# Strassen's seven products in the first feed-forward matrix of a diffusion backbone step

## The chip, the cores and the metric

One core of a Trainium2 chip. TensorE multiplies (weights are loaded into it, the tokens stream past and the sums land in PSUM), VectorE and ScalarE do the elementwise work and alone of the two sides read PSUM, gpsimd (POOL in the profile) does elementwise work in SBUF and issues some DMAs, and SyncE (SP) issues the others. The metric is the time of one execution on the device in microseconds; lower is better.

## The reference, cut to what matters

Two trunk layers over 640 tokens (512 of a latent grid and 128 of context), 1024 features. A layer is a feed-forward half-step, a token-mixing step (state-space scan, attention, gated MLP) and a second feed-forward half-step; each is preceded by a norm with modulation vectors worked out from a condition.

```python
D_MODEL, SEQ, DEC_SEQ, DEPTH, D_FF = 1024, 128, 512, 2, 2816
def swiglu_ffn(h, w_in, w_out):
    gate, up = jnp.split(h @ w_in, 2, axis=-1)      # w_in: 1024 x 5632, "the first matrix"
    return (jax.nn.silu(gate) * up) @ w_out
def adaln(cond, w_ada, b_ada):
    mod = jax.nn.silu(cond) @ w_ada + b_ada
    return mod.reshape(cond.shape[0], N_MOD, D_MODEL)
def trunk_layer(x, mod, lp, ctx_kv, ssm_init):
    h = modulate(rmsnorm(x, lp['norm_ffn1']), sh1, sc1)
    x = x + 0.5 * g1 * swiglu_ffn(h, lp['ffn1_w_in'], lp['ffn1_w_out'])
    h = modulate(rmsnorm(x, lp['norm_mix']), sh2, sc2)
    mix, ctx_state = token_mixing(h, lp, ctx_kv, ssm_init)
    x = x + g2 * mix
    h = modulate(rmsnorm(x, lp['norm_ffn2']), sh3, sc3)
    x = x + 0.5 * g3 * swiglu_ffn(h, lp['ffn2_w_in'], lp['ffn2_w_out'])
    return x, ctx_state
```

So there are four feed-forward stages: layer 0 first and second, layer 1 first and second. They are called the first to the fourth (or last) stage here.

## The kernel before, in words

Features lie on the 128 partitions, tokens along the columns. The 640 tokens are two halves, `HALF` (line 27): A has 384, B has 256. Float32 accuracy comes from three passes: every operand is kept as a high part in the matmul's format and a low part (the remainder), and `mm3` (line 361) issues high by high, high by low and low by high, at lines 365 to 367. The splitting is `split_h` (line 188): ScalarE writes the high part (line 191), VectorE subtracts it from the source (line 192). Normed tokens are in `H`, high and low.

A feed-forward stage (`ffn_items`, line 566) goes by 22 units of 128 hidden features. For a unit and a half, `in_task` (line 598) runs eight tiles of 128 features for the gate, ScalarE takes its SiLU out of PSUM (line 610), eight tiles for the up part follow, VectorE multiplies (line 619) and the result is split into `hid`. Units come in four blocks, `BLOCKS` (line 30), of 5, 5, 6 and 6. After a block's units (its *in-phase*) come its `out_task`s (line 681; the *out-phase*): for each of eight output tiles and each half, the block's units are multiplied by the second matrix and `accumulate` (line 389) adds the result, times its gate vector, to the residual `x` on VectorE (line 395; A is one range of columns, B two).

The order of all engines' instructions is laid down at build time. `run` (line 92) walks a list of tasks; `clock` (line 80) advances a clock `T` of the matrix work by a set length for each `mm3` (`MM3`, line 44) and lets background generators go on when their time on that clock has come. Weights come in chunks of 1024 columns (512 KB): `dma` (line 110) loads them on SP's queue into two raw buffers, `split` (line 125) splits them into one of seven buffers, at most 24 units of `T` ahead of use (`LEAD`), 4.5 while a norm is under way (`LEAD_HOT`).

In the background of the first three stages run: `ada` (line 237), which works out modulation vectors with two VectorE instructions of 1024 columns a step (line 260), at a pace in `T` given in `build` (4.5 then 7.0 in the first stage, 48 steps; 4.5 then 6.5 in the second, 56 steps; 10.0 in the third, 24 steps; none in the fourth); and in the first and third `ssm_build` (line 774), which works out tables of the state-space part on VectorE and gpsimd and sends them to memory with gpsimd's DMAs. `norm` (line 297) runs, tile by tile, when a half's residual is done: VectorE and gpsimd scale, ScalarE shifts and rounds, VectorE takes the remainder. `square` (line 284) sums squares on ScalarE and gpsimd. At the very start, `opening` (line 405) loads the tokens and works out the first norm, with modulation on VectorE (line 449) and gpsimd (line 469) side by side, while `lead_task` (line 638) runs the first two units feature tile by feature tile. PSUM has four banks for products (tag `mm`) and two each of two small tags.

## Time and profile before

| | us |
|---|---|
| median of 3 runs | 2525.57 (2521.89 to 2526.12) |
| the profiled execution, span | 2522.3 |
| first stage, 85 to 534.5 | 449.5 |
| second stage, 824 to 1290 | 466 |
| third stage, 1290 to 1768 | 478 |
| fourth stage, 2054 to 2522 | 468 |
| mixing steps | 289.5 and 286 |

The profile is of one execution. Times count from its first instruction. A *window* gives each engine's busy time in a stretch, with the granted clock of TensorE (1.00 is full speed). A line of the list of instruction groups gives line, engine, operation, output and inputs by the program's names, shape, count, busy time with the mean of one in ns, and the idle time ahead of it with what ended it. A line of the timeline gives start and duration of instructions in order of time. A busy span on VectorE counts a wait of an instruction that has been started; a matmul's span includes its way through the array, so that successive ones overlap.

### The profile page before, as it was taken

To read this page: it belongs to the slowest core of one execution; us is meant where nothing else is said; L and a number is where in the kernel's file an instruction comes from. 1 tells how busy PE (TensorE), PEld (TensorE's weight loads), DVE (VectorE), ACT (ScalarE), POOL (GpSimd) and SP (SyncE) were. 2 spreads that over 40 slices of the span, in tenths; PEclk is the share of its full clock that TensorE was granted. 3 is DMA by queue.
4 is the path that set the end of the run, shared out by engine and by line. 5 is a ranking of instruction groups with operands and counts; after the bars stand their busy time and mean duration, and the time that the engine had idled before them with its cause. 6 is when DMAs were issued, how large, how long until landed. Compare 5 with 4: busy or idle time off the path is not lost.

```text
span 2522.3 us, 44229 instructions
## 1 busy us (share of the span) xinstructions
PE 2466.4 (98%) x17428; PEld 2408.2 (95%) x17428; DVE 1555.2 (62%) x3293; ACT 812.4 (32%) x1689; POOL 680.9 (27%) x1520
## 2 busy tenths in 40 slices
PE   6999999999999999999999999999999999999999
PEld 5999999998988999999999999999998889999999
DVE  7798777557566776666568675534685764343332
ACT  5322222254444422222242222223545452222121
POOL 5105765623342000000020566551253320000000
PEclk8999999999999999999999999999999999999999
DMA  6445454325341344443324344332444212222222
GB/s 229 144 147 170 159 168 164 109 110 148 121 129 46 127 172 142 151 148 144 117 86 144 134 150 151 105 98 74 143 149 122 82 54 91 74 85 67 83 68 67
DMA packets 102115, 307.29 MB, mean 122 GB/s; under 512 B 21666, under 2 KB 24834, under 8 KB 101524
## 3 DMA queue, kind: packets, MB, share of 16 engines
q1 hardware_dynamic: 86548, 254.92, 29.8%
q0 software_dynamic: 15360, 49.56, 6.2%
q8 instruction: 137, 2.24, 0.4%
q14 instruction: 70, 0.57, 0.1%
HBM read 281.78 MB, written 23.17 MB: 121 GB/s over the span
## 4 chain that ended last, share of the span: by engine, by line
PE 87%; DVE 5%; issue 3%; ACT 2%; POOL 1%; DMA 1%; SPq 0%; DVEq 0%; POOLq 0%; ACTq 0%
PE mm L365 26%; PE mm L367 26%; PE mm L366 26%; PE mm L1389 1%; PE mm L1390 1%; PE mm L1391 1%; DVE aj L449 1%; DVE w L192 1%; PE sA L1258 1%; PE sB L1280 1%; PE mm L1227 1%; DMA T<-dT 0%; DVE H L541 0%; PE sB L1093 0%; PE sA L909 0%
## 5 line engine op out<-in xcount | busy, mean ns | idle before, releaser
L365 PE MATMUL mm<-H,w 128*128 128x384 f32 (+1 forms) x3248 | 1021.3, 314 | 9.5 <-ACT H L536 5.6
L366 PE MATMUL mm<-H,w 128*128 128x384 f32 (+1 forms) x3248 | 1011.9, 312 | 12.3 <-DVE H L541 9.3
L367 PE MATMUL mm<-H,w 128*128 128x384 f32 (+1 forms) x3248 | 1011.3, 311 | 0.0
L365 PEld LDWEIGHTS mm<-H,w 128*128 128x128 f32 x3248 | 615.0, 189 | 21.9 <-issue 13.8
L366 PEld LDWEIGHTS mm<-H,w 128*128 128x128 f32 x3248 | 615.1, 189 | 15.5 <-DVE H L541 11.1
L367 PEld LDWEIGHTS mm<-H,w 128*128 128x128 f32 x3248 | 614.7, 189 | 1.1 <-DVE w L192 1.1
L192 DVE TENSOR_TENSOR w<-r,w 128x1024 fp32r<-128x1024 f32 (+2 forms) x354 | 395.5, 1119 | 243.7 <-ACT w L191 242.3
L365 PE MATMUL mm<-hid,w 128*128 128x384 f32 (+1 forms) x1408 | 434.4, 309 | 0.0
L367 PE MATMUL mm<-hid,w 128*128 128x384 f32 (+1 forms) x1408 | 433.5, 308 | 0.0
L366 PE MATMUL mm<-hid,w 128*128 128x384 f32 (+1 forms) x1408 | 432.9, 307 | 0.0
L191 ACT ACTIVATE w<-r 128x1024 fp32r<-128x1024 f32 (+2 forms) x354 | 337.8, 956 | 289.8 <-PE mm L367 232.5
L260 DVE SCALAR_TENSOR_TENSOR aj<-ar,sbc 128x1024 bf16<-128x1024 f32 x256 | 317.4, 1240 | 36.4 <-DMA ar<-w_ada 32.4
L395 DVE SCALAR_TENSOR_TENSOR x<-mm,mod,x 128x128 f32<-128x128 f32 (+1 forms) x480 | 194.0, 434 | 183.7 <-PE mm L367 183.0
L365 PEld LDWEIGHTS mm<-hid,w 128*128 128x128 f32 x1408 | 264.1, 188 | 1.0 <-issue 1.0
L366 PEld LDWEIGHTS mm<-hid,w 128*128 128x128 f32 x1408 | 264.7, 188 | 0.0
L367 PEld LDWEIGHTS mm<-hid,w 128*128 128x128 f32 x1408 | 264.5, 188 | 0.0
L191 ACT ACTIVATE hid<-sg 128x384 fp32r<-128x384 f32 (+1 forms) x176 | 82.9, 471 | 550.4 <-DVE sg L619 534.5
L295 POOL TENSOR_TENSOR acc<-acc,sq 128x384 f32<-128x384 f32 (+1 forms) x60 | 53.7, 895 | 604.8 <-ACT sq L293 604.1
L619 DVE TENSOR_TENSOR sg<-sg,mm 128x256 f32<-128x256 f32 (+1 forms) x161 | 78.1, 485 | 212.0 <-PE mm L367 211.9
L610 ACT ACTIVATE sg<-mm 128x256 f32<-128x256 f32 (+1 forms) x161 | 70.0, 435 | 329.7 <-PE mm L367 329.7
L192 DVE TENSOR_TENSOR hid<-sg,hid 128x384 fp32r<-128x384 f32 (+1 forms) x176 | 89.2, 507 | 94.6 <-ACT hid L191 94.6
L1389 PE MATMUL mm<-w,H 128*128 128x256 f32 x480 | 143.1, 298 | 0.0
(329 smaller groups left out, 2642.2 us busy)
## 6 DMA issues: line engine op xcount, KB each, us to landing
ar<-w_ada SPq DMA_DIRECT2D x128, 512.0 KB, 4.5
r<-f1i SPq DMA_DIRECT2D x88, 512.0 KB, 3.4
r<-f0i SPq DMA_DIRECT2D x86, 512.0 KB, 3.5
r<-f0o SPq DMA_DIRECT2D x32, 384.0 KB, 3.1
r<-wqkv SPq DMA_DIRECT2D x24, 512.0 KB, 3.5
r<-f1o SPq DMA_DIRECT2D x32, 384.0 KB, 3.0
r<-f0o SPq DMA_DIRECT2D x32, 320.0 KB, 2.9
r<-f1o SPq DMA_DIRECT2D x32, 320.0 KB, 2.9
```

The source lines that it names most:

```text
L191: self.nc.scalar.activation(hi, src, AF.Copy)
L192: self.nc.vector.tensor_tensor(lo, src, hi.bitcast(F32), op=ALU.subtract)
L260: nc.vector.scalar_tensor_tensor(jk, r, 1.0, self.sbc[:, c, :], op0=ALU.mult, op1=ALU.mult, accum_out=m[:, c, j * KD + k:j * KD + k + 1])
L295: eng.tensor_tensor(self.acc[X], self.acc[X], q, op=ALU.add)
L365: nc.tensor.matmul(out, hi, rhs_hi, start=start, stop=False)
L366: nc.tensor.matmul(out, hi, rhs_lo, start=False, stop=False)
L367: nc.tensor.matmul(out, lo, rhs_hi, start=False, stop=stop)
L395: nc.vector.scalar_tensor_tensor(self.x[:, m, r0:r1], p[:, r0 - s:r1 - s], self.mod[l][:, c, g * KD + m:g * KD + m + 1], self.x[:, m, r0:r ...
L449: v.scalar_tensor_tensor(jk, r, 1.0, self.sbc[:, c, :], op0=ALU.mult, op1=ALU.mult, accum_out=m[:, c, j:j + 1])
L610: nc.scalar.activation(sg[:, :e - s], p[:, :e - s], AF.Silu)
L619: nc.vector.tensor_tensor(sg[:, :e - s], sg[:, :e - s], p[:, :e - s], op=ALU.mult)
L1389: nc.tensor.matmul(p[:, :256], H[:, 0, k, ts], wh, start=k == 0, stop=False)
```

## The change

The first matrix of a feed-forward stage is multiplied by Strassen's scheme (in Winograd's form): the two halves of the 1024 features, the two halves of the tokens and the pair of gate and up are the two-by-two blocks. In place of eight block products for a unit (gate and up, two feature halves, two token halves) there are seven, each of four feature tiles of 128 by 320 token columns.

- Halves are both 320 tokens (`HT`); A is one range of columns for modulation, B is 192 and 128.
- Four operands on the weights' side are sums of 512 columns: s1 = p0 + p1, s2 = s1 + g0, s4 = s2 + g1, s3 = g0 + p0 (g and p for gate and up, 0 and 1 for the feature half). gpsimd adds them; each is then split as other weights are, so that seven operands of 512 columns are split for a unit.
- Four operands on the tokens' side (t1 to t4) are worked out once a stage from the four blocks of the normed tokens, in `x_sums`, on VectorE and gpsimd, four rounds, behind the second half's norm. In the first stage the first two units are multiplied as before, and `all_x_sums` follows them.
- The seven tasks of a unit are `p1` to `p7`. Three banks of PSUM are accumulated on further after their intermediate value has been read: VectorE and ScalarE combine the products (five operations from PSUM on VectorE, two multiplications, two remainders; ScalarE one copy, two SiLUs, two high parts).
- Weights come in pieces of 512 columns (256 KB) in 24 buffers, at most 7 of them raw and 3 sums. A sum is issued at most 13 units of `T` ahead of use, its high part 9 ahead (7 and 4.5 while a norm is under way), the remainder 0.6 after the high part.
- Six blocks of 4, 4, 4, 4, 3 and 3 units in place of four. In stages two to four the first four units start with the products that need half A alone, from pieces that are loaded a second time for it (`EARLY`).
- The tables of the state-space part keep their work; gpsimd's is spread by more yields. The buffers of the normed tokens are shared with the mixing step's, and the scratch for gpsimd's DMA descriptors is set to 8192.

```diff
-HALF = {"A": (0, 384), "B": (384, 640)}
-BLOCKS = ((0, 5), (5, 5), (10, 6), (16, 6))
+HT = 320
+HALF = {"A": (0, HT), "B": (HT, 2 * HT)}
+BLOCKS = ((0, 4), (4, 4), (8, 4), (12, 4), (16, 3), (19, 3))
+EARLY = 4
-LEAD, LEAD_HOT, DMA_LAG, SPLIT_GAP = 24.0, 4.5, 3.5, 2.0
+LEAD, LEAD_HOT, DMA_LAG = (13.0, 9.0), (7.0, 4.5), 3.5
+SUM_GAP, HIGH_GAP, SUM_TO_HIGH, HIGH_TO_LOW = 1.3, 0.7, 1.4, 0.6
+NW, NRAW, NSUM = 24, 7, 3
...
+        def take():
+            c = order[st["a"]]
+            n, x, y = self.ops[c]
...
+                nc.gpsimd.tensor_tensor(total[c][:, :n], source(x, n), source(y, n), op=ALU.add)
...
+        def low():
+            c = order[st["l"]]
...
+            nc.vector.tensor_tensor(lo[:, :n], src, hi[:, :n].bitcast(F32), op=ALU.subtract)
...
+    def x_sums(self, k, r12, r22):
...
+        v.tensor_tensor(t1, h11, r12, op=ALU.subtract)
+        g.tensor_tensor(t3, r12, r22, op=ALU.subtract)
+        v.tensor_tensor(t1, t1, l11, op=ALU.add)
+        v.tensor_tensor(t2, r22, t1, op=ALU.add)
+        g.tensor_tensor(t4, h21, t2, op=ALU.subtract)
+        g.tensor_tensor(t4, t4, l21, op=ALU.add)
...
+        def p5(w, u):
+            bank["c", u] = self.ps()[:, :HT]
+            self.product(bank["c", u], w, "t1", True)
+            v.tensor_tensor(temp((u, "c")), bank["c", u], tmp[u, "p"], op=ALU.add)
+        def p6(w, u):
+            bank["b", u] = self.ps()[:, :HT]
+            self.product(bank["b", u], w, "t2", True)
+            v.tensor_tensor(temp((u, "b")), bank["b", u], tmp[u, "p"], op=ALU.subtract)
...
+        def p7(w, u):
+            self.product(bank["b", u], w, "t3", False)
+            a, b = tmp[u, "b"], tmp[u, "c"]
+            v.tensor_tensor(b, bank["b", u], b, op=ALU.subtract)
+            def rest():
+                v.tensor_tensor(b, a, b, op=ALU.mult)
+                drop((u, "b"))
+                high(u, "B", (u, "c"))
+                self.later(2, lambda: low(u, "B", (u, "c")))
+            self.later(2, rest)
+        def p4(w, u):
+            p = bank.pop(("b", u))
+            self.product(p, w, "t4", False)
+            a, b = tmp[u, "a"], tmp[u, "p"]
+            v.tensor_tensor(b, p, b, op=ALU.subtract)
+            v.tensor_tensor(b, a, b, op=ALU.mult)
+            drop((u, "a"))
+            high(u, "A", (u, "p"))
+            self.later(2, lambda: low(u, "A", (u, "p")))
...
+            for n, u in enumerate(us):
+                if u not in early:
+                    items.append(task(p1, u, "11"))
+                items.append(task(p5, u, "s1"))
+                if n:
+                    items.append(task(p4, us[n - 1], "22"))
+                items.append(task(p6, u, "s2"))
+                if u not in early:
+                    items.append(task(p2, u, "12"))
+                items.append(task(p3, u, "s4"))
+                items.append(task(p7, u, "s3"))
+            items.append(task(p4, us[-1], "22"))
...
+            self.ops[op("s1")] = (512, r["p0"], r["p1"])
+            self.ops[op("s2")] = (512, ("o", op("s1")), r["g0"])
+            self.ops[op("s4")] = (512, ("o", op("s2")), r["g1"])
+            self.ops[op("s3")] = (512, r["g0"], r["p0"])
...
-                yield 14.0
+                yield 3.0
...
-    nc = bacc.Bacc("TRN2", target_bir_lowering=False, num_devices=1)
+    nc = bacc.Bacc("TRN2", target_bir_lowering=False, num_devices=1, dynamic_dma_scratch_size=8192)
```

## Rows read from the trace of the kernel before

**Rows 1.** The page: span, busy time by engine, chain that ended last by engine.
```profile
span 2522.3 us, 44229 instructions
...
PE 2466.4 (98%) x17428; PEld 2408.2 (95%) x17428; DVE 1555.2 (62%) x3293; ACT 812.4 (32%) x1689; POOL 680.9 (27%) x1520
...
PE 87%; DVE 5%; issue 3%; ACT 2%; POOL 1%; DMA 1%; SPq 0%; DVEq 0%; POOLq 0%; ACTq 0%
```

**Rows 2.** Windows: the four stages; length, busy time by engine (instructions), clock, DMA.
```profile
85.00:534.50 449.50, 449.50 (x3103) 445.91 (x3101) 333.58 (x676) 115.06 (x194) 213.12 (x522) 1.00 0.45 151
...
824.00:1290.00 466.00, 466.00 (x3174) 465.87 (x3173) 305.86 (x551) 124.78 (x207) 12.56 (x15) 1.00 0.39 137
1290.00:1768.00 478.00, 476.96 (x3286) 473.10 (x3284) 295.64 (x632) 137.19 (x234) 200.50 (x532) 1.00 0.36 121
...
2054.00:2522.00 468.00, 464.68 (x3164) 464.47 (x3162) 170.48 (x298) 111.49 (x185) 2.19 (x3) 1.00 0.23 74
```

**Rows 3.** Windows: in- and out-phases of stage two, four (five units), one (six).
```profile
929.50:1000.20 70.70, 70.70 (x483) 70.70 (x482) 45.67 (x76) 17.18 (x30) 0.00 (x0) 1.00 0.37 131
1000.20:1035.20 35.00, 35.00 (x243) 35.00 (x242) 26.97 (x51) 7.10 (x8) 0.00 (x0) 1.00 0.54 189
2159.40:2230.00 70.60, 70.60 (x482) 70.60 (x481) 21.77 (x32) 17.17 (x30) 0.00 (x0) 1.00 0.20 63
2230.00:2264.90 34.90, 34.90 (x243) 34.90 (x242) 16.34 (x30) 7.09 (x8) 0.00 (x0) 1.00 0.29 101
272.40:360.30 87.90, 87.90 (x610) 86.62 (x609) 66.03 (x116) 23.44 (x41) 55.43 (x133) 1.00 0.48 157
360.30:403.90 43.60, 43.60 (x307) 43.12 (x306) 35.33 (x68) 8.54 (x11) 26.49 (x78) 1.00 0.51 182
```

**Rows 4.** Instruction groups of VectorE, shapes apart, 2100 to 2500 (quiet).
```profile
L192 DVE TENSOR_TENSOR w<-r,w 128x1024 fp32r<-128x1024 f32 x34 | 41.5, 1222 | 39.3 <-ACT w L191 39.3
L395 DVE SCALAR_TENSOR_TENSOR x<-mm,mod,x 128x384 f32<-128x384 f32 x28 | 17.3, 618 | 45.8 <-PE mm L367 45.8
L395 DVE SCALAR_TENSOR_TENSOR x<-mm,mod,x 128x128 f32<-128x128 f32 x56 | 17.0, 346 | 24.9 <-PE mm L367 24.9
...
L192 DVE TENSOR_TENSOR w<-r,w 128x640 fp32r<-128x640 f32 x15 | 12.4, 825 | 22.5 <-ACT w L191 22.3
L192 DVE TENSOR_TENSOR hid<-sg,hid 128x384 fp32r<-128x384 f32 x19 | 10.6, 558 | 11.2 <-ACT hid L191 11.2
L619 DVE TENSOR_TENSOR sg<-sg,mm 128x384 f32<-128x384 f32 x19 | 10.5, 555 | 40.9 <-PE mm L367 40.9
L192 DVE TENSOR_TENSOR hid<-sg,hid 128x256 fp32r<-128x256 f32 x19 | 8.1, 426 | 9.2 <-ACT hid L191 9.2
```

**Rows 5.** Timeline of VectorE, first stage: start, duration, instruction.
```profile
169.81 1.22 DVE L192 TENSOR_TENSOR w<-r,w 128x1024 fp32r<-128x1024 f32 x1
170.94 1.22 DVE L260 SCALAR_TENSOR_TENSOR aj<-ar,sbc 128x1024 bf16<-128x1024 f32 x1
...
172.09 0.27 DVE L820 SCALAR_TENSOR_TENSOR ang<-ang 128x112 f32<-128x112 f32 x1
```

**Rows 6.** Instruction groups of VectorE over the span: modulation in the background, in the opening.
```profile
L260 DVE SCALAR_TENSOR_TENSOR aj<-ar,sbc 128x1024 bf16<-128x1024 f32 x256 | 317.4, 1240 | 36.4 <-DMA ar<-w_ada 32.4 <-ACT sbc L252 2.7
...
L449 DVE SCALAR_TENSOR_TENSOR aj<-ring,sbc 128x1024 bf16<-128x1024 f32 x16 | 30.9, 1934 | 0.3
```

**Rows 7.** Instruction groups of gpsimd over the span: the adds of squares.
```profile
L295 POOL TENSOR_TENSOR acc<-acc,sq 128x384 f32<-128x384 f32 x30 | 30.5, 1016 | 538.2 <-ACT sq L293 538.0
...
L295 POOL TENSOR_TENSOR acc<-acc,sq 128x256 f32<-128x256 f32 x30 | 23.3, 775 | 66.6 <-ACT sq L293 66.1
```

**Rows 8.** Timelines of gpsimd and of VectorE in the opening.
```profile
32.08 2.75 POOL L469 TENSOR_TENSOR prod<-ring,sbc 128x1024 f32<-128x1024 f32 x1 [3.73 <-ACT prod L474]
...
42.14 3.46 POOL L469 TENSOR_TENSOR prod<-ring,sbc 128x1024 f32<-128x1024 f32 x1 [4.84 <-ACT prod L474]
...
32.51 3.40 DVE L449 SCALAR_TENSOR_TENSOR aj<-ring,sbc 128x1024 bf16<-128x1024 f32 x1
...
42.15 1.22 DVE L449 SCALAR_TENSOR_TENSOR aj<-ring,sbc 128x1024 bf16<-128x1024 f32 x1
```

**Rows 9.** Instruction groups of VectorE in the loaded in-phase, 272.4 to 360.3.
```profile
L619 DVE TENSOR_TENSOR sg<-sg,mm 128x384 f32<-128x384 f32 x6 | 3.3, 551 | 4.5 <-PE mm L367 4.5
L192 DVE TENSOR_TENSOR hid<-sg,hid 128x256 fp32r<-128x256 f32 x5 | 2.7, 535 | 2.4 <-ACT hid L191 2.4
```

More of the change, by code (lines that the diff above doesn't have):

```diff
@@ new lines, in read, with over @@
+        def read(x):
+            if x[0] == "r":
+                users[x[1]] -= 1
+                if not users[x[1]]:
+                    raw.pop(x[1])
+                    free.append(slot.pop(x[1]))
+                    dma()
+        def over(c):
+            if c in total and place[c] < st["l"] and all(place[d] < st["a"] for d in sums.get(c, ())):
+                total.pop(c)
+                free.append(slot.pop((c, "t")))
+                dma()
+        def take():
+            c = order[st["a"]]
+            n, x, y = self.ops[c]
+            st["a"] += 1
+            t_sum[c] = self.T
+            if y:
+                total[c] = new((c, "t"), F32)
+                nc.gpsimd.tensor_tensor(total[c][:, :n], source(x, n), source(y, n), op=ALU.add)
+                st["sum"] = self.T
+                read(x)
+                read(y)
+                if x[0] == "o":
+                    over(x[1])
@@ L142, in run, with have @@
+        def have(ops):
+            dma()
+            while any(place[c] >= st["l"] for c in ops):
+                if st["l"] < st["h"]:
+                    low()
+                elif st["h"] < st["a"]:
+                    high()
+                else:
+                    take()
+            return [pair[c] for c in ops]
+        self.dma, self.splitter, self.get = dma, splitter, have
         for i, it in enumerate(items):
-            st["i"] = i
             if it[0] == "call":
@@ L149, in run @@
             else:
[L150 to L153 removed]
+                it[2](have(it[1]))
             for c in it[1]:
                 if last[c] == i:
[L156 removed]
+                    pair.pop(c)
+                    free.extend((slot.pop((c, 0)), slot.pop((c, 1))))
+                    dma()
     def rsqrt(self, y, a):
@@ L368, in mm3, with product, together @@
         self.clock(MM3[rhs_hi.shape[-1]])
-    def together(self, w, X, done):
+    def product(self, out, w, name, start, ks=range(4)):
+        hi, lo = self.xop(name)
+        for k in ks:
+            while self.xr[name] < min(4, k + 2):
+                self.advance(self.norms["A" if name in ("11", "21") else "B"])
+            self.mm3(out, w, slice(k * 128, k * 128 + 128), hi[:, k], lo[:, k], start and k == 0, k == 3, True)
+    def together(self, c, w, h, X, ps, done):
         s, e = HALF[X]
-        ps = [self.ps() for _ in w]
@@ new lines, in high, with low, p1 @@
+        def high(u, X, src):
+            hid[u, X] = [new((u, X, i), F32R) for i in range(2)]
+            nc.scalar.activation(hid[u, X][0], tmp[src], AF.Copy)
+        def low(u, X, src):
+            a, b = hid[u, X]
+            v.tensor_tensor(b, tmp[src], a.bitcast(F32), op=ALU.subtract)
+            drop(src)
+        bank = {}
+        def p1(w, u):
+            bank["a", u] = self.ps()[:, :HT]
+            self.product(bank["a", u], w, "11", True)
+            nc.scalar.activation(temp((u, "p")), bank["a", u], AF.Copy)
@@ L667, in fn @@
[L667 to L685 removed]
+                            products(k, w)
```

722 lines of the change are left out of this document (441 added, 281 removed).

## The prediction

> **What bounds the kernel now.** I read the page's busy table and its chain first: TensorE is busy for 98% of the span and holds 87% of the chain that ended last [rows 1]. So time is matmul time, unless another engine takes over. Next the stretches: a window for each of the four feed-forward stages [rows 2]. In the last one, with no modulation vectors and no state-space tables beside it, VectorE is busy 170 us of 468; in the first 334 of 450, and gpsimd, idle in the second and the last, is at 213 and 200 us in the first and third. The reader is to see that the four stages have one and the same matmul work and very different cover. Then single phases [rows 3]: in the quiet stage the in-phase of five units takes 70.6 us, 14.12 a unit, with VectorE busy 4.35 us a unit, and the out-phase of five takes 34.9, 6.98 a unit. The second stage has the same lengths though VectorE does twice as much: it has room now. The question is how much room is left afterwards.
>
> The change is priced per *cycle*: four units of the in-phase and their out-phase. Before: 4 x 14.12 + 27.9 = 84.4 us. With state-space tables beside it some 88: the loaded in-phase of six took 87.9 against 6 x 14.12 = 84.7, the out-phase 43.6 against 41.9 [rows 3], their own small products.
>
> **TensorE.** Seven products for eight: 14.12 x 7/8 = 12.35 us a unit. Halves of 320 are not in the trace; 384 and 256 columns together make the rate measured, and two of 320 are as many, so I take the same. Out-phase as before (same columns, six blocks instead of four). Saving 1.765 us x 86 units (22 a stage, the opening's two stay plain) = 152 us, 5.5 cycles a stage (5 in the first) of 49.4 + 27.9 = 77.3 us.
>
> **VectorE.** Its forms come from a quiet window [rows 4], less what overlaps: of two large ones in a row, a 1.22 us instruction is followed by the next after 1.13 to 1.15 us [rows 5], so 0.08 comes off each. 640 columns then cost 0.745, 384 cost 0.478, hence by their slope 0.61 for 512 and 0.41 for 320; the product out of PSUM is as long as one in SBUF at 384 columns, so 0.41 too. Residual updates: 384 cost 0.54, 128 cost 0.266, so 0.47 for 320 and 0.335 for 192. Per unit the change has seven weight remainders of 512 (before: two of 1024) and nine operations of 320 (five subtract, or add, with PSUM; two multiply; two remainders): 7 x 0.61 + 9 x 0.41 = 8.0 us, against 4.35. An out-phase of four: 8 x (0.61 + 0.47 + 0.335 + 0.266) = 13.5 us. So a quiet cycle has 32 + 13.5 us of VectorE in 77.3: fine by itself. What comes on top in the loaded stages stays in the code as it was: a modulation step is two instructions of 1.15 us [rows 5, 6], paced by the program's clock, which counts 0.41 for a three-pass step: 4 x 28 x 0.41 = 45.9 units in the in-phase, 8 x 2 x 4 x 0.41 = 26.2 in the out-phase, 398 in a stage. At pace 6.5 (second stage) that is 16.2 and 9.3 us, at 7 (first) 15.1 and 8.6, at 10 (third) 10.6 and 6.0. The state-space tables: third stage less last is 125 us of VectorE [rows 2], 48 modulation instructions are 60 of it [rows 6], so some 62 us in 478: 6.4 in an in-phase, 3.6 in an out-phase.
>
> The Trainium skill, VectorE: DVE Perf Modes, sections The TRN2 errata and The DRAIN you can't avoid, gives (N+151)/0.96 ns for such an instruction and, where it is held, a next start only behind the emptied pipe. As an estimate by it a unit would hold 7 x 0.69 + 9 x 0.49 = 9.25 us, 5 us more an in-phase. The start-to-start times above disagree with the second half of it, and the sum goes by them.
>
> **gpsimd's sums.** Four of 512 columns a unit. Its adds of 384 and 256 columns take 1.016 and 0.775 us [rows 7], so 1.26 us by slope, 5 us a unit: it has the time. What decides is whom they hold up. In the opening gpsimd's 2.75 us product starts 0.43 us ahead of VectorE's modulation instruction, and this takes 3.40 instead of 1.22; later VectorE is 10 ns short of simultaneous, keeps its 1.22, and gpsimd's product takes 3.46 [rows 8]. The same VectorE form has a mean of 1934 ns in the opening and 1240 elsewhere [rows 6]. In the loaded in-phase, gpsimd busy 63%, the remainder of 256 columns grows from 426 to 535 ns while the product that reads PSUM stays at 551 [rows 4, 9]. So an instruction with two SBUF inputs and a gpsimd one exclude each other, whole instruction by whole instruction; one that reads PSUM passes. The Trainium skill, SBUF — State Buffer, section Who interferes with whom, says so too, as an exclusive lock on a shared pair of ports; it is the one rule I found that speaks against putting the sums on gpsimd, and the trace agrees with it.
>
> Bounds of a sum's price to VectorE: 0 (it falls into a gap or beside PSUM reads) and 1.26 us (whole). The opening's instance loses 2.18 us to an operation of 2.75, which is 1.0 us for one of 1.26; the other instance there loses nothing [rows 8], and in the loaded in-phase a remainder loses 0.11 on average [rows 4, 9]. I take 0.8 us, 12.8 a block of sixteen, nearer to the opening's, since VectorE will be nearly as full as there. The tables' own gpsimd operations, spread wider by the new yields, I put at 4 us an in-phase and 2 an out-phase (0 to 8).
>
> **Who then waits.** Behind a remainder that waits for gpsimd stand, in VectorE's order, the PSUM subtractions: product p7 accumulates on what p6's subtraction has read, two tasks (3.5 us) later, p4 likewise after p7. Once VectorE is that far behind, TensorE goes at its pace. On ScalarE the high part of a sum waits for gpsimd, and the copy and the SiLU that free banks queue behind it. On SP the weight loads come in twice as many halves, behind modulation loads that wait for VectorE; the eight early pieces more a stage are nothing. On gpsimd the sums queue behind the tables' work and its DMA issues.
>
> In-phase by stage, VectorE against TensorE, less 2 us (0 to 4) of sums that the lead of 13 pulls into the out-phase:
> - Last: 32 + 12.8 = 44.8 against 49.4. TensorE-bound: -7.1 x 5.5 = -39. Two losses are new: a block's last p4 stands right behind p7 (a subtraction and its hand-offs, 0.5 to 2, I take 1.2, six times: 7), and at the entry the second half's norm is followed by four rounds of operand sums (six VectorE operations of 0.41 and four gpsimd ones of 0.9 each, 24 us in a row, against 14 us of products in the four early units; I take 9, 0 to 15). Sum -23.
> - Second: 32 + 16.2 + 12.8 - 2 = 59.0, out-phase 27.9: 86.9 against 84.4 for 8 x 4.5 + 48 x 6.5 = 348 of 398 clock units, 4.8 cycles: +12; the rest -5; entry +9: +16.
> - Third: 32 + 10.6 + 6.4 + 12.8 + 4 - 2 = 63.8, out 29.4: 93.2 against 88 for 240 of 398, 3.3 cycles: +17; without modulation 82.6: -12; entry +9: +14.
> - First: 32 + 15.1 + 6.4 + 12.8 + 4 - 2 = 68.3, out 29.7: 98 against 88 for 316 of 380, 4.15 cycles: +41; rest -5; operand sums behind the opening +10: +46.
>
> Sum +53 us. On the profiled execution's span of 2522.3 [rows 1] that is 2575; the median shown is 2525.57, 3.3 above the span, so **2579 us**. The mixing stages keep their work.
>
> **Rivals.** *A, the sums fall into gaps:* at price 0 the in-phases are 48.2 (second), 49 (third) and 53.5 (first), TensorE-bound but for the first: -23, -23, -23, -8, together -77, 2448 us. For it: the last stage leaves two thirds of VectorE's time free [rows 3], and sums run well ahead of need. Against: [rows 8]. The total turns where a sum costs VectorE about 0.47 us. *B, gpsimd becomes the bound:* in the first and third stage a table's operations and sums each wait for VectorE; if a wait is 1 us instead of 0.5, sums come late and ScalarE stops in front of its bank copies; some 8 us on nine cycles, 2650 us. Against it: gpsimd has 200 busy us in 478 now [rows 2]. *C, no overlap on VectorE:* if each of the sixteen operations of a unit holds its engine for its whole duration, 0.08 x 16 x 4 = 5 us come on 15 VectorE-bound in-phases, 2655 us; [rows 5] speak against it. It is what the section on the DRAIN would make of this kernel. That the change doesn't compute by seven products I see no sign of.
>
> **Chances.** Forecast 0.50 (its own range 2515 to 2630, from the sum's price 0.45 to 1.1 and entries of 0 to 15), A 0.37, B 0.08, C 0.05. The part of the forecast's range between 2520 and 2531 is the 0.05 of "same" (0.2%, 5 us, is about what a measurement of this kernel can tell from no change). Faster 0.37 (A), same 0.05, slower 0.58. Range 2430 to 2655: A's centre and C's end are in it.
>
> **What would show it.** Right: the last feed-forward stage at some 445 us, the first at 490 or more; VectorE above 90% busy in the first three; weight remainders of 512 with means well above 0.69 us beside gpsimd adds above 1.26; TensorE's idle time released by VectorE. Wrong: remainders near 0.69, all four stages near 440 (A); ScalarE waiting for gpsimd (B). I am also wrong if entries cost tens of us, or if idle TensorE lowers its granted clock from 1.00.

## The result, and the profile after

The changed kernel takes **2866.94 us** (2863.75 to 2870.49) against 2525.03 in the same rounds: 1.1355 times as long, 95% interval 1.1339 to 1.1371. Predicted were 2579 us, in a range up to 2655: the sign was right, the size far off. The page of after, against [rows 1]; under the busy times, the clock granted in 40 slices of the span:

```profile
span 2868.7 us, 46399 instructions
...
PE 2468.0 (86%) x16420; PEld 2369.7 (83%) x16420; DVE 2236.4 (78%) x4552; ACT 1058.1 (37%) x2409; POOL 1270.1 (44%) x1928
...
PEclk9798999897999979999997999999999997999999
```

TensorE has 1008 instructions fewer and no less busy time: spans stretch at the lower clock (a product of 320 columns spans 0.31 us at full clock and 0.64 at the lower one). It is idle for 14% of the span. VectorE has 681 us more, gpsimd 589. (The chain that ended last can't be compared with that of [rows 1]: here the page follows it back only to 2214 us.) What TensorE waits for most, over the span (us in total, times, longest):

```profile
PE mm L581 <- DVE hid L873: 85.4, 37, 6.3
PE mm L581 <- DVE hid L885: 69.5, 38, 6.2
PE mm L581 <- ACT hx L543: 65.3, 12, 7.4
```

The first two are the subtractions of p6 and p7 that the prediction named, the third is a round of operand sums.

Windows of after, cut at the start of each norm of half A (first stage, mixing, second, third, mixing, fourth); the columns are those of [rows 2]:

```profile
85.00:677.10 592.10, 466.62 (x2857) 450.20 (x2856) 495.11 (x955) 167.20 (x342) 333.37 (x559) 0.89 0.37 116
677.10:973.90 296.80, 270.12 (x2143) 249.70 (x2144) 184.37 (x533) 135.27 (x403) 113.06 (x263) 0.94 0.36 108
973.90:1519.00 545.10, 472.82 (x2989) 460.30 (x2989) 494.97 (x867) 193.78 (x392) 177.96 (x125) 0.93 0.39 128
1519.00:2096.20 577.20, 477.84 (x3025) 459.76 (x3026) 470.07 (x931) 196.83 (x405) 351.96 (x628) 0.92 0.32 101
2096.20:2376.80 280.60, 267.79 (x2143) 246.71 (x2144) 184.24 (x533) 135.38 (x403) 102.40 (x212) 0.97 0.38 113
2376.80:2868.60 491.80, 453.45 (x3000) 447.47 (x2999) 344.35 (x634) 185.93 (x375) 151.21 (x116) 0.96 0.25 79
```

All stages below are cut like this (in us; Δ is after less before). The loss is in the three stages that have other work beside the products, and the fourth doesn't gain:

| | before | after | Δ | Δ predicted | no weight sums | weight sums on VectorE | no operand sums | neither |
|---|---|---|---|---|---|---|---|---|
| first | 442.9 | 592.1 | +149 | +46 | 504.3 | 537.4 | 562.0 | 482.2 |
| mixing | 280.9 | 296.8 | +16 | 0 | 291.7 | 292.7 | 292.6 | 293.7 |
| second | 474.7 | 545.1 | +70 | +16 | 488.5 | 525.3 | 524.7 | 468.3 |
| third | 478.1 | 577.2 | +99 | +14 | 505.7 | 531.9 | 556.9 | 489.8 |
| mixing | 277.1 | 280.6 | +4 | 0 | 279.6 | 280.2 | 280.0 | 280.4 |
| fourth | 483.5 | 491.8 | +8 | -23 | 481.2 | 486.8 | 472.1 | 462.9 |

Then single phases of after, against [rows 3]: an in-phase of four units of the second stage and of the fourth, the first stage's third in-phase and the third's fourth, both beside modulation and tables, the fourth's entry (from its first norm to its first out-phase), an out-phase of the second:

```profile
1211.50:1271.00 59.50, 51.93 (x336) 50.65 (x336) 56.83 (x91) 21.24 (x44) 19.60 (x12) 0.97 0.45 144
2511.50:2561.60 50.10, 49.42 (x337) 49.19 (x337) 35.81 (x61) 22.27 (x45) 15.73 (x11) 1.00 0.31 96
301.00:375.00 74.00, 57.95 (x350) 55.39 (x349) 61.82 (x105) 23.45 (x49) 51.77 (x88) 0.91 0.41 131
1858.50:1930.80 72.30, 57.71 (x362) 54.56 (x361) 58.55 (x100) 24.27 (x51) 46.71 (x90) 0.93 0.38 121
2376.80:2483.30 106.50, 75.48 (x432) 70.93 (x432) 82.19 (x154) 52.17 (x114) 50.42 (x44) 0.82 0.26 82
1271.10:1299.20 28.10, 28.10 (x194) 28.10 (x193) 27.07 (x53) 7.32 (x13) 6.51 (x5) 1.00 0.37 124
```

Two of them are as predicted: 59.5 us (59.0), VectorE 96% busy, and 50.1 (49.4), TensorE busy throughout. The misses are the rows with tables, 74.0 and 72.3 where the sum gave 68.3 and 63.8, and the entry, 106.5 where it gave 73.6 (before it is 85.8 from norm to out-phase; less 70.6 for five units, plus 49.4 and 9). Note the fourth row: no engine is above 81%. It has modulation in it, as the window of line L385 alone shows (each modulation instruction leaves a second, short record). Tables without modulation stand beside the third stage's two blocks of three units; the first takes 40.5 us (second line), the next 47.5, where three quarters of the sum's 53.2 are 39.9. The last line is the first stage's second in-phase, the longest of its kind, with VectorE busy 95% of it and gpsimd 31%:

```profile
1858.50:1930.80 72.30, 11.87 (x19) 0.93 0.38 121
1959.10:1999.60 40.50, 38.49 (x266) 37.60 (x264) 31.13 (x60) 16.69 (x35) 31.70 (x70) 1.00 0.36 113
192.00:270.40 78.40, 58.16 (x338) 56.21 (x337) 74.13 (x189) 22.86 (x47) 24.72 (x19) 0.86 0.34 111
```

That a gpsimd sum shuts VectorE out shows in the groups of VectorE, 1123 to 1520 of after, where a remainder of 512 columns was 0.69 us by the slope of [rows 4]:

```profile
L219 DVE TENSOR_TENSOR w<-w 128x512 fp32r<-128x512 f32 x150 | 131.3, 880 | 6.9 <-POOL w L198 3.1 <-ACT w L210 2.3 <-issue 1.2
...
L888 DVE TENSOR_TENSOR hid<-hid 128x320 f32<-128x320 f32 x18 | 16.4, 912 | 0.1
...
L900 DVE TENSOR_TENSOR hid<-hid 128x320 f32<-128x320 f32 x18 | 8.9, 492 | 0.6
...
L868 DVE TENSOR_TENSOR hid<-mm,hid 128x320 f32<-128x320 f32 x18 | 8.7, 484 | 0.3 <-PE mm L583 0.3
```

All three work on 320 columns; L888 and L900 multiply two inputs in SBUF, L868 adds one in PSUM. It is not the form alone that costs time, but what gpsimd does at that moment: by the timeline seven of the eighteen L888 overlap a gpsimd instruction and take 1580 ns on average, the other eleven 486, and no L900 overlaps one. Of the operations that read PSUM many overlap one too (eight of the eighteen of L885) and all stay at some 483 ns. (The Trainium skill, SBUF — State Buffer, section Who interferes with whom, states this lock; the rows agree.)

### The profile page after: what moved, and what is told of

Its sections match the earlier page's. It is cut to its first block, busy times and chain, and to the rows that moved or that the text cites. A ratio compares the mean times of both kernels' runs of the same rounds, so it can differ in the third digit from the quotient of the medians.

```text
span 2868.7 us, 46399 instructions
## 1 busy us (share of the span) xinstructions
PE 2468.0 (86%) x16420; PEld 2369.7 (83%) x16420; DVE 2236.4 (78%) x4552; ACT 1058.1 (37%) x2409; POOL 1270.1 (44%) x1928
## 5 line engine op out<-in xcount | busy, mean ns | idle before, releaser
L581 PE MATMUL mm<-hx,w 128*128 128x320 f32 x2904 | 965.4, 332 | 310.1 <-DVE hid L873 85.4
L582 PE MATMUL mm<-hx,w 128*128 128x320 f32 x2904 | 943.6, 325 | 14.4 <-DVE hx L758 11.4
L583 PE MATMUL mm<-hx,w 128*128 128x320 f32 x2904 | 938.4, 323 | 1.8 <-DVE w L219 1.8
L581 PEld LDWEIGHTS mm<-hx,w 128*128 128x128 f32 x2904 | 583.1, 201 | 355.0 <-DVE hid L873 76.5
L198 POOL TENSOR_TENSOR w<-w 128x512 f32<-128x512 f32 x344 | 520.1, 1513 | 804.4 <-PE mm L582 293.3
L219 DVE TENSOR_TENSOR w<-w 128x512 fp32r<-128x512 f32 (+1 forms) x906 | 733.7, 817 | 157.5 <-ACT w L210 100.9
L210 ACT ACTIVATE w<-w 128x512 fp32r<-128x512 f32 (+1 forms) x906 | 537.4, 615 | 653.4 <-DVE w L219 214.6
L582 PEld LDWEIGHTS mm<-hx,w 128*128 128x128 f32 x2904 | 584.7, 201 | 21.0 <-DVE hx L758 12.5
L583 PEld LDWEIGHTS mm<-hx,w 128*128 128x128 f32 x2904 | 583.6, 201 | 2.1 <-DVE w L219 2.1
L581 PE MATMUL mm<-hid,w 128*128 128x320 f32 x1408 | 441.1, 313 | 17.5 <-DVE x L619 17.2
L582 PE MATMUL mm<-hid,w 128*128 128x320 f32 x1408 | 438.0, 311 | 0.0
L583 PE MATMUL mm<-hid,w 128*128 128x320 f32 x1408 | 437.6, 311 | 0.0
L385 DVE SCALAR_TENSOR_TENSOR aj<-ar,sbc 128x1024 bf16<-128x1024 f32 x256 | 347.2, 1356 | 9.3 <-DMA ar<-w_ada 6.6
L619 DVE SCALAR_TENSOR_TENSOR x<-mm,mod,x 128x128 f32<-128x128 f32 (+2 forms) x672 | 269.8, 432 | 89.8 <-PE mm L583 88.0
L845 ACT ACTIVATE hid<-hid 128x320 fp32r<-128x320 f32 x176 | 83.0, 472 | 416.5 <-DVE hid L888 228.7
L849 DVE TENSOR_TENSOR hid<-hid 128x320 fp32r<-128x320 f32 x176 | 108.2, 615 | 51.3 <-ACT hid L845 50.9
L1740 PE MATMUL mm<-w,hx 128*128 128x256 f32 x480 | 144.5, 301 | 0.0
L1741 PE MATMUL mm<-w,hx 128*128 128x256 f32 x480 | 138.0, 288 | 0.0
L1742 PE MATMUL mm<-w,hx 128*128 128x256 f32 x480 | 137.8, 287 | 0.0
```

The source lines that it names most:

```text
L198: nc.gpsimd.tensor_tensor(total[c][:, :n], source(x, n), source(y, n), op=ALU.add)
L210: nc.scalar.activation(pair[c][0][:, :n], src, AF.Copy)
L219: nc.vector.tensor_tensor(lo[:, :n], src, hi[:, :n].bitcast(F32), op=ALU.subtract)
L385: nc.vector.scalar_tensor_tensor(jk, r, 1.0, self.sbc[:, c, :], op0=ALU.mult, op1=ALU.mult, accum_out=m[:, c, j * KD + k:j * KD + k + 1])
L581: nc.tensor.matmul(out, hi, rhs_hi, start=start, stop=False, skip_group_check=parts)
L582: nc.tensor.matmul(out, hi, rhs_lo, start=False, stop=False, skip_group_check=parts)
```

## The experiments

**1. The price of a weight sum.** Two kernels: one replaces each summed block by a raw one, one lets VectorE do the sums.

```diff
-            self.ops[op("s1")] = (512, r["p0"], r["p1"])
+            self.ops[op("s1")] = (512, r["p0"], None)     # and s2, s3, s4 likewise
```

> Leaves out the gpsimd sums of weight blocks: each summed weight is replaced by one of its raw blocks, so no product is Strassen's any more; TensorE, the high and low parts, the loads and the operand sums stay. Theory 1 (a gpsimd sum holds VectorE back by about 0.8 us, and tables and sums hold each other up on gpsimd): the in-phase of the second stage goes from 59.5 us to 50, TensorE-bound; those of the first and third, 67 to 78 us now, come down to 55 or less; the entries into the stages (operand sums) stay as they are. Time about 2680 us (2620 to 2740). Theory 2 (the sums cost VectorE next to nothing, it is simply full with its own remainders and subtractions): the second stage's in-phase stays above 56 us and the time above 2800 us.

```diff
-                nc.gpsimd.tensor_tensor(total[c][:, :n], source(x, n), source(y, n), op=ALU.add)
+                nc.vector.tensor_tensor(total[c][:, :n], source(x, n), source(y, n), op=ALU.add)
```

> The same sums of weight blocks, computed by VectorE instead of gpsimd: 0.61 us each, start to start. Theory 1 (a gpsimd sum holds VectorE back by some 0.8 us): VectorE gains 0.2 us a sum, so the second stage's in-phase of sixteen sums goes from 59.5 to some 56.5 us, and the first and third, where sums also queue behind the tables on gpsimd, gain 5 to 12 us an in-phase; time 2740 to 2830 us. Theory 2 (a sum on gpsimd costs VectorE less than 0.47 us): VectorE's load rises by 0.15 to 0.6 us a sum, the second stage's in-phase is 62 us or more, time 2880 us or more.

Measured: 2637.83 and 2741.00 us. Windows of the first kernel, the same in-phases of the second, the first and the third stage:

```profile
1096.00:1146.10 50.10, 49.42 (x338) 49.19 (x337) 47.00 (x92) 21.30 (x44) 0.00 (x0) 1.00 0.54 181
277.20:334.30 57.10, 53.38 (x349) 52.49 (x348) 52.04 (x104) 21.74 (x46) 32.30 (x71) 0.94 0.51 166
1665.50:1719.70 54.20, 52.28 (x361) 50.76 (x361) 47.40 (x94) 22.86 (x49) 31.45 (x77) 1.00 0.49 158
```

The same three of the second kernel:

```profile
1143.50:1199.70 56.20, 50.53 (x337) 49.21 (x337) 54.56 (x106) 21.51 (x44) 0.00 (x0) 1.00 0.45 155
288.20:350.20 62.00, 53.11 (x349) 51.43 (x349) 59.91 (x117) 22.56 (x47) 36.15 (x72) 0.97 0.45 147
1755.70:1815.60 59.90, 54.32 (x362) 52.35 (x361) 57.55 (x110) 24.18 (x51) 38.05 (x77) 0.97 0.44 146
```

Theory 1 both times. Of a block's sixteen sums eleven or twelve start in the in-phase, the others in the out-phase, where TensorE is the bound. In the second stage VectorE is busy 47.0 us without sums, 54.6 with twelve of its own (0.63 us each) and 56.8 with eleven or twelve on gpsimd: 0.82 to 0.89 us a sum, where I took 0.8. It isn't one price for all stages: in the fourth, where VectorE has room, the first kernel has it busy 31.8 us in an in-phase and after 35.8, 0.36 us for each of eleven sums. And beside modulation and tables the step from gpsimd to VectorE is worth 12 us an in-phase, not 3, though VectorE's busy time hardly changes (58.6 and 57.6 us in the third stage): with the sums on gpsimd VectorE stands idle for 13.8 us of that in-phase, with its own for 2.4. What it then waits for is in part 4. VectorE is the better place for the sums in every stage, in the fourth too (486.8 against 491.8).

**2. The operand sums.** One kernel leaves the rounds out, one gives their gpsimd part to VectorE, one leaves out both kinds of sums.

```diff
-        v.tensor_tensor(t1, h11, r12, op=ALU.subtract)
-        ...
+        yield 0.1          # x_sums only says that the blocks are there; t1, t2, t3, t4 stand for 11, 21, 22, 22
```

> Leaves out the four rounds of operand sums of each stage (x_sums): the products that would use them read the plain blocks instead, so no product is Strassen's any more; weight sums and everything else stay. Theory 1 (the entry into a stage is a serial chain of VectorE, gpsimd and ScalarE of four rounds, and TensorE waits for it): the fourth stage's first in-phase goes from about 100 us to 60 or 65, the second's and third's lose as much, the first stage's opening 20 to 30, and the granted clock in these stretches goes back up; time about 2720 us (2680 to 2760). Theory 2 (the entries are long because of the second half's norm and the first weights): each entry gains under 15 us, time above 2800 us.

```diff
-        nc, v, g = self.nc, self.nc.vector, self.nc.gpsimd
+        nc, v, g = self.nc, self.nc.vector, self.nc.vector      # in x_sums
```

> The four gpsimd operations of a round of operand sums go to VectorE (0.41 us each by their form instead of about 1.0 us, and no handing over in between); weight sums stay on gpsimd. Theory 1 (a round is a serial chain, and gpsimd's part of it some 2 to 3 us of 6.4 to 7.6): a round takes 4.5 to 5.5 us, an entry 6 to 10 us less, time 2835 to 2850 us. Theory 2 (VectorE is full in the entries, it is its queue that sets a round's length): a round stays above 6 us, time 2860 us or more.

> Leaves out both kinds of sums, those of weight blocks (gpsimd) and those of operands (the four rounds of a stage): the products read raw and plain blocks, so none is Strassen's. What is left has TensorE's work of seven products, and VectorE's subtractions out of PSUM. Theory 1 (the two are separate costs at separate places): the gains of the two runs that left out one each add up, 2867 - 229 - 92 = about 2546 us (2530 to 2570), and the granted clock's mean is 0.97 or more. Theory 2 (both are the same waits, so that either removal takes most of what there is): 2600 us or more.

Measured: 2775.09, 2849.38 and 2564.07 us. The first lies between the two theories: each stage loses 20 to 30 us, not 38. The fourth stage's entry goes from 106.5 to 86.8 us without rounds, to 95.9 without weight sums, to 77.5 without either: 20 + 11, and 13 stay that neither accounts for. Without either the time is near the sum of the single gains, 2546, with a clock of 0.967. Even so it is 39 us above the kernel before, though TensorE has seven products for eight: the fourth stage gains 21 us, the first loses 39. What a round is, in after's fourth entry; first TensorE, then gpsimd, then VectorE, from timelines:

```profile
2431.48 0.64 PE L581 MATMUL mm<-hx,w 128*128 128x320 f32 x1 [5.94 <-ACT hx L543]
...
2438.85 0.64 PE L581 MATMUL mm<-hx,w 128*128 128x320 f32 x1 [5.94 <-ACT hx L543]
```
```profile
2431.53 1.15 POOL L536 TENSOR_TENSOR xt<-hx,xt 128x320 f32<-128x320 f32 x1 [1.88 <-DVE xt L535]
2432.75 0.99 POOL L537 TENSOR_TENSOR xt<-xt,hx 128x320 f32<-128x320 f32 x1
```
```profile
2434.28 0.64 DVE L553 TENSOR_TENSOR hx<-xt,hx 128x320 fp32r<-128x320 f32 x1 [1.25 <-ACT hx L543]
2434.84 0.66 DVE L491 SCALAR_TENSOR_TENSOR xn<-x,mod,sB 128x192 f32<-128x192 f32 x2
2436.55 0.82 DVE L503 SCALAR_TENSOR_TENSOR hx<-xn,hx 128x320 fp32r<-128x320 f32 x1 [1.06 <-ACT hx L499]
```

TensorE does three products and waits 5.94 us, every 7.37 us. Between two rounds stand the norm's own pieces (L491, L503), which I had not counted. With everything on VectorE a round still takes some 6.5 us, and VectorE is then 88% busy; its window over 30 us of rounds:

```profile
2395.00:2425.00 30.00, 11.21 (x33) 8.22 (x32) 26.42 (x55) 15.22 (x35) 5.88 (x5) 0.50 0.05 17
```

So theory 2 of that run holds in stages two to four (0.5 to 3 us less each), though its time lies in theory 1's range: most of its 18 us is from the first stage (11) and the mixing behind it (4.5).

**3. The tables' pace.**

```diff
-                yield 3.0
+                yield 14.0          # and none of the new pauses within a table
```

> The state-space tables' steps are spread as in the kernel before (14.0 at the end of a table instead of 3.0, without the new pauses: 32.5 units of the program's clock a table instead of 37.5). Theory 1 (the stage's clock counts fewer units with seven products, the tables ask for more, so what is left over is run in one piece ahead of the mixing stage's norm): the two gaps of TensorE at the first mixing stage's start (9.0 and 16.2 us) go, the mixing stage takes some 290 us instead of 317, and time falls by 10 to 30 us. Theory 2 (the tables are late because gpsimd is late): the gaps stay, and bunched table steps cost the first and third stage 10 to 30 us more; time 2870 to 2900 us.

Measured 2932.99 us: both theories are half right. Ahead of the first mixing stage after's TensorE stands still; waits of TensorE, 655 to 700 (us in total, times, longest):

```profile
PE mm L581 <- ACT hx L495: 16.0, 1, 16.0
PE sA L1258 <- DVE CL L1244: 8.7, 1, 8.7
```

With the old pace these gaps are gone and the mixing stage is at 282.5 us. So the new pauses (37.5 clock units a table for 32.5), with fewer units in a stage (398 for some 430), leave tables over, which run in one piece ahead of the norm. But in the stages bunched steps cost more than that: third stage 626.0 for 577.2.

**4. What is it beside the tables?** The expectations call the third stage's in-phase of 72.3 us one without modulation; that is wrong, in each of these runs ten modulation instructions stand in it (12 us of VectorE in after). Five kernels: sums begun earlier; the tables' powers left out; three kinds of the tables' DMA issues moved later in gpsimd's queue; that with earlier sums; those issues given to other queues.

```diff
-LEAD, LEAD_HOT, DMA_LAG = (13.0, 9.0), (7.0, 4.5), 3.5
+LEAD, LEAD_HOT, DMA_LAG = (20.0, 9.0), (7.0, 4.5), 3.5
-NW, NRAW, NSUM = 24, 7, 3
+NW, NRAW, NSUM = 24, 7, 6
```

> Weight sums are begun up to 20 instead of 13 units of the program's clock ahead of their use, and up to six instead of three of them may wait for their high and low parts; nothing else is changed. Theory 1 (in the first and third stage sums stand late in gpsimd's queue behind the tables, and ScalarE and VectorE wait in order for the late sum: a matter of lateness): a longer lead takes the lateness out, the in-phases of the first and third stage come down from 67 to 78 us to 60 to 66 (the runs with sums on VectorE gave 58 to 64), time 2770 to 2820 us. Theory 2 (gpsimd and VectorE have no more time to give, together: a matter of throughput): they stay within 3 us, time 2850 us or more. The second stage's in-phase, 59.5 us, stays by either.

```diff
-                gp_.memset(T[:, 0, :, 0], 1.0)
-                ...                              # twelve copies, five complex products
+                gp_.memset(T, 1.0)
+                yield 9.0
```

> Leaves out the powers of the state-space tables on gpsimd (twelve copies and thirty small products a table, 13 us of gpsimd's time each by the third stage's groups, some 1.2 tables an in-phase); one fill with ones stands for them, the pauses stay. Theory 1 (the sums wait in gpsimd's queue behind the tables, and the two shut VectorE out in turn): the third stage's in-phase without modulation goes from 72.3 us to 60 or 65, those of the first and third with modulation fall by 6 to 12 us; the second and fourth stage stay; time 2770 to 2820 us. Theory 2 (VectorE is the bound by its own work, and what gpsimd does beside it matters little): in-phases within 3 us, time 2850 us or more.

```diff
-                    gp_.dma_start(S["T2"][qq, :, o:o + 288] ...
-                yield 8.0
+                yield 4.0
+                    gp_.dma_start(S["T2"][qq, :, o:o + 288] ...   # strip and ET likewise, a pause later
+                yield 4.0
```

> Three kinds of DMA issues of the state-space tables in gpsimd's queue (of CL, strip and ET) are moved behind the next pause of the program, so that what they send has been written by then; nothing is left out. Theory 1 (gpsimd stands in order in front of an issue whose data ScalarE or VectorE has not written yet, 17 us in the third stage's in-phase without modulation, with the sums behind it, and ScalarE in turn stands in front of the late sum: the engines' queues lock step): these waits go, that in-phase comes down from 72.3 us to 60 to 65 and those with modulation by 4 to 10 us, time 2760 to 2820 us. Theory 2 (the throughput of gpsimd and VectorE together is used up, the waits only fill what is left): in-phases within 3 us, time 2850 us or more.

> The same moved issues, and sums begun up to 20 units of the program's clock ahead with up to six waiting. Theory 1 (lateness in order, now from both sides): the in-phases of the first and third stage are within 3 us of those with sums on VectorE (62, 62, 58 and 60), time 2740 to 2790 us. Theory 2 (throughput): as in the run with earlier sums alone, 2850 us or more.

```diff
-                    gp_.dma_start(S["T2"][qq, :, o:o + 288] ...
+                    nc.sync.dma_start(S["T2"][qq, :, o:o + 288] ...   # the strip too; ET by nc.scalar.dma_start
```

> The same three kinds of the tables' DMA issues leave gpsimd's queue altogether: ET's goes to ScalarE's queue, behind ScalarE's own copy, CL's and the strip's to SyncE's, among the weight loads; the run with moved issues had left 14 of 17 us of gpsimd's waits in place. Theory 1 (gpsimd stands in order in front of these issues, the sums behind it): gpsimd's waits go, the third stage's in-phase without modulation comes down from 72.3 to 60 to 65 us, time 2780 to 2830 us. Theory 2 (the throughput of gpsimd and VectorE together is used up; the waits stand in time that would be lost anyway): in-phases within 4 us, time 2845 us or more.

| | time | third stage, fourth in-phase | first stage, third in-phase |
|---|---|---|---|
| after | 2866.9 | 72.3 | 74.0 |
| sums earlier | 2860.4 | 69.9 | 70.5 |
| no powers of tables | 2803.4 | 66.3 | 67.9 |
| issues later | 2858.2 | 69.7 | 69.6 |
| issues later, sums earlier | 2841.1 | 68.3 | 68.9 |
| issues on other queues | 2844.3 | 70.1 | 66.1 |
| sums on VectorE | 2741.0 | 59.9 | 62.0 |

Each row is one execution, but for the first, whose four lie between 2863.75 and 2870.49. In the trace of after it looks like queue order: in the 72.3 us ScalarE waits 24.5 us for late sums, VectorE 11.5 of its 13.8 idle us for a late sum or the high part behind it, and gpsimd waits in front of issues whose data ScalarE or VectorE has yet to write (a third, the strip's, is another 3.3 us). Waits of ScalarE and VectorE, then of gpsimd, in that window (us in total, times, longest):

```profile
ACT w L210 <- POOL w L198: 24.5, 7, 6.6
...
DVE w L219 <- POOL w L198: 7.2, 2, 4.3
DVE w L219 <- ACT w L210: 4.3, 2, 4.0
```
```profile
POOL dT L1273 <- ACT ET L1272: 8.8, 1, 8.8
POOL dT L1251 <- DVE CL L1248: 5.1, 1, 5.1
```

Moving the issues later left 14 of those 17 us in place. With the issues on other queues they are gone, and the in-phase stays:

```profile
1836.00:1906.10 70.10, 56.61 (x361) 53.54 (x360) 58.02 (x99) 23.27 (x49) 61.50 (x121) 0.95 0.41 133
```

gpsimd's busy time goes from 46.7 to 61.5 us in place of the waits: it has more of the tables' instructions in this window (121 for 90), and its small ones are longer (a table's copy, L1282, takes 474 ns, in after's window 348). ScalarE still waits 13.9 us for sums, and VectorE is idle 12. So theory 2 by its signs, but for the first stage's in-phase: queue order at these issues is worth 2 to 8 us an in-phase. The run with both moved issues and earlier sums lies between its theories (2841, where they had 2790 and 2850). In every run with the sums on gpsimd VectorE stands idle 8 to 14 us in the third stage's in-phase, with the sums on VectorE 2. So sums come late there whatever their place in the queue; that the two engines' locking each other out makes gpsimd too slow for both jobs fits this, but no run shows it by itself. Leaving out the powers takes 10 us from gpsimd's busy time in this in-phase and shortens it by 6 (its time is in theory 1's range), moving the sums to VectorE by 12. The 66.3 us without powers are compared with the sum's 63.8 less up to 4 for the tables' gpsimd work; what the 3 to 7 us above it are stays open.

**5. The clock.** Two kernels give TensorE idle products where it waits: 30 at ten waits for rounds; 8 ahead of three products of each unit in the first and third stage.

```diff
+            if n > 1 and name not in ("11", "21"):
+                idle = self.ps("sA")[:, :HT]
+                for _ in range(FILL):     # 30
+                    nc.tensor.matmul(idle, w[0][:, :128], self.xop("11")[0][:, 0], start=True, stop=True)
```

> Nothing of the change is left out; at ten places where TensorE waits for a round of operand sums (three in each of the second, third and fourth stage, one in the first) it gets 30 idle products of 320 columns into a bank that nobody reads, 4.0 us at 133 ns each. Theory 1 (after a wait of 6 to 7 us the clock falls to half and the next products take twice as long): the granted clock in these entries is 1.00 or near it, their products go every 148 ns instead of 270 to 290, and each entry gets 5 to 10 us shorter though TensorE does more; time 2835 to 2855 us. Theory 2 (the half clock in the entries is hidden behind the rounds, which set the end): entries as long as before, time 2860 to 2880 us.

> In the first and third stage three of a unit's seven products are each led by 8 idle products of 320 columns into their own bank (1.06 us at 133 ns, 12.8 us an in-phase of four units), which fit into the time that TensorE waits there. Theory 1 (the half clock, a third of these in-phases, makes the products late and holds up VectorE, which waits for them): the granted clock rises from 0.90 towards 1.00 and the in-phases of 67 to 78 us get 3 to 6 us shorter, time 2830 to 2855 us. Theory 2 (the half clock falls into time that TensorE would wait anyway): the clock rises, and the in-phases stay or grow by up to the 12.8 us; time 2865 to 2930 us.

Measured: 2859.57 and 2895.41 us. Theory 2 both times. In the first kernel the fourth stage's granted clock goes from 0.96 to 0.98 and its length from 491.8 to 492.1; the second stage's from 0.93 to 0.96, 545.1 to 542.9. In the second the first stage's in-phase goes from 0.91 to 0.96 and from 74.0 to 77.4 us, the third's from 0.93 to 0.95 and from 72.3 to 73.1, for 96 idle products, 14 us at the 147 ns that one takes at full clock (not 133, as I had written): TensorE had most of that time. So in these stretches the lower clock goes with a TensorE that waits, and raising it shortened no stage by more than some 3 us. What it costs by itself isn't separated, as the idle products take time too.

**6. Where it could pay.** Seven products in blocks two to six of the fourth stage alone, and, last, the change as it is with all sums on VectorE and the tables a little denser.

```diff
+        sums = (l, f) == (1, 1)
...
+            elif not sums or b == 0:
+                plain_units(us, us[:n_early] if b == 0 else [])
...
+            if sums and b == 0:
+                items.append(("call", lambda: self.norms.update(B=self.spawn(self.all_x_sums(), 0.0, True))))
```

> Seven products only where VectorE has room, in blocks two to six of the fourth feed-forward stage (18 of its 22 units); all other units take the plain eight products, without any sums, and the four rounds of operand sums of the fourth stage run beside the first block's out-phase. Theory 1 (what the change loses lies in the entries and in the stages with modulation and tables): 18 x 1.765 = 32 us less than the kernel before, less some 4 us of block ends: about 2497 us (2485 to 2515), with the granted clock near 0.99. Theory 2 (the sums and rounds hold TensorE up wherever they stand): 2525 us or more.

> All sums on VectorE, those of weight blocks and those of operands, and the pause at the end of a state-space table 0.5 instead of 3.0 units of the program's clock, so that the eight tables end some 20 units earlier; the seven products stay in all four stages. Theory 1 (the three costs lie at different places, so that their cures add up: 126 us for the weight sums, 18 for the rounds, 10 to 25 for the tables left over at the first mixing stage): 2867 - 126 - 18 - 15 = about 2708 us (2690 to 2725). Theory 2 (with VectorE doing all sums it is itself the bound everywhere, and tables that are denser cost what they give back): 2735 us or more. By either it stays slower than the kernel before, 2525.

Measured: 2595.92 us (1.0284, 1.0267 to 1.0301) and 2716.72 us (1.0757, 1.0738 to 1.0776). The second adds up as its theory 1 says. The first is a miss. Its blocks of seven products take what they should (50.2 and 28.2 us for four units), but the first out-phase, which has the rounds beside it, does not:

```profile
2188.40:2233.60 45.20, 35.36 (x194) 33.17 (x193) 39.73 (x66) 13.12 (x28) 22.95 (x21) 0.81 0.10 34
```

45.2 us for 28, with VectorE 88% busy; the fourth stage is at 480.6, 3 us under before. And the three plain stages are 20 to 25 us longer than before's in this layout of six blocks and equal halves with its own entries: in the second the entry takes 81.6 us instead of 85.9 less one unit, 71.8, and the first out-phase 34.3 instead of 27.9. In the fourth the entry takes 78.3 for 71.7. So the layout alone, without any sums, accounts for 7 to 10 of the 13 us that were left over at the entry in part 2. No version here beats the kernel before.

## Why the prediction was wrong

Right: *TensorE's* 49.4 and 27.9 us (50.1 and 28.1); in the second stage *VectorE's* load and the *price of a sum* (in-phase 59.0 predicted, 59.5; 0.8 a sum, measured 0.82 to 0.89); rival C fails with them (a modulation instruction of 1.21 us is still followed by the next start after 1.14); rival A fails, as a sum costs more there than the 0.47 us at which it would have turned. The value between the bounds 0 and 1.26 came from the opening's instance [rows 8], and it was the right neighbour for a nearly full VectorE. Some of the 59.5 for 59.0 is luck: the sum had VectorE busy throughout, and it is busy 56.8 us and idle 2.7. In the quiet fourth stage a sum costs 0.36 and VectorE is busy 35.8 us for 44.8 predicted, which changes nothing, as TensorE is the bound there.

Wrong, in order of size, as excess over the prediction's own terms:

- **The entry, "I take 9, 0 to 15".** Measured from norm to first out-phase: fourth 106.5 for 73.6, that is 33 more; second 119.7 for 83.3 (85.9 - 70.6 + 59 + 9), 36 more; third 108.2 for 81.8 (79.6 - 70.6 + 63.8 + 9), 26 more; the opening's in-phase 125.5 for 93.5 (101.1 less a unit of 14.1 and two eighths of one, plus 10), 32 more. Some **127 us**. The working took 24 us of rounds in a row against 14 us of early products. A round is 7.4 us, not 6: hand-offs, and the norm's own two pieces of that feature tile, which stand in the same queue. And the weight sums go on beside it (11 us in the fourth), and the new layout costs 7 to 10 us there by itself, which the sum put at nothing. The prediction named this as a sign of being wrong: "if entries cost tens of us".
- **"The tables' own gpsimd operations I put at 4 us an in-phase", and rival B at 0.08.** In-phases of the first and third stage: first 78.3, 74.0, 70.8 for 68.3; third 66.8, 70.0, 72.3 for 63.8, together 36 us; with the blocks of three (29) and the out-phases (20) some **85 us**. The first of them is another miss: gpsimd is busy only 24.7 us of it, VectorE 74.1, as the set-up of the tables on VectorE stands there in one piece (some 15 us, where I had spread it at 6.4 an in-phase). In the others sums come late and ScalarE and VectorE stand in front of them, which is B's mechanism and the sign that the prediction gave for it. I priced the lock for the sums against VectorE alone and put no wait for a late sum into the in-phase. gpsimd at 200 busy us of 478 [rows 2], my evidence against B, was a busy time without that competition. Why the sums are late stays open in part, as part 4 says.
- **"The mixing stages keep their work."** The tables' new pauses against a stage with fewer clock units: 8.7 + 16.0 = **25 us** of TensorE's time ahead of the first mixing stage. Both numbers were in the diff and in my own count of 398 units; I never added up the tables' pauses.
- **The clock at 1.00.** It fell, as the last sentence of the prediction feared: 411 us of the span at the lower level (1.2 GHz) against 42 before. Raising it by idle products shortened no stage by more than some 3 us; how much of the excess above is its work isn't separated.

The rest of the 288 us, some 50, is spread over the other phases and hand-overs between stages, and wasn't taken apart.

## What to carry to other kernels

An engine with free time is no free engine: what a second elementwise engine costs the first is measured on the shape and the stage at hand, and if an addition costs a nearly full VectorE 0.85 us on gpsimd and 0.63 on VectorE itself, it belongs on VectorE. Look also at what stands idle: the larger loss here was not longer instructions but engines that waited in order for a late sum. Count a serial start-up step with every instruction that stands between its rounds in the same queues, and add up what paced background work asks for against the clock units that are left when the main work shrinks. Fewer products pay only where their preparation has room: here one stage of four had it, and its entry took the gain.

## What was not expected of the hardware

gpsimd's small instructions stretch beside a busy VectorE as VectorE's do beside gpsimd: the same copy of two columns takes 289 ns on average before and 311 after, and in the third stage's fourth in-phase 348 in after and 469 with the sums on VectorE, which is then 96% busy. A TensorE that was fed idle products had a higher granted clock (0.96 for 0.91 in the first stage's in-phase) and the in-phase was no shorter (77.4 us for 74.0).
